# An expert's gather and add over 128 rows instead of 104, with the ranks dealt over the partitions

## The chip, the core and the metric

The kernel runs on one core of one Trainium2 chip. The metric is device time in microseconds (us), the median of several runs. Engines are called PE (TensorE matmul), PEld (its weight loads), DVE (VectorE), ACT (ScalarE), POOL (GpSimd) and SP (SyncE). DMAs issued on SP go through the hardware queue q1, those issued on POOL through the software queue q0; both are worked off by the same 16 transfer engines.

## What is computed

One layer on 1,024 tokens of width 1,024 in float32: an input projection, a stick-breaking attention and a gated recurrence side by side, an output projection, and then a mixture of 32 experts, on which the change bears. A router gives every token two experts; the tokens of an expert are gathered, run through the expert, weighted and added back:

```
grp = argmax(softmax(x2 @ w_rg + b_rg)); in_grp = (x2 @ w_re + b_re)[group grp]
top_val, top_idx = top_k(in_grp, 2); gate = softmax(top_val) * p_grp
for each block of an expert's tokens:
    xb = x2[tok]
    hb = silu(xb @ w_gate[e]) * (xb @ w_up[e])        # 1024 -> 512
    y[tok] += (hb @ w_down[e]) * gate                 # 512 -> 1024
out = rmsnorm(h + y) * g_final
```

With the reference's inputs the 2,048 assignments give an expert between 41 and 82 tokens, 64 on average (counted by running the reference's router); expert 0 has 76, expert 30 has 56, expert 31 has 66.

## The kernel before

**Slots.** Every expert has `C = 104` slots. `place` (L832 on) works out the rank of each token among those of its expert, and a one-hot comparison of the rank with `iota` (L844) turns it into a slot: slot number = rank = partition. `idx[slot, e]` then holds the token's row number; a slot that no token has holds 1024. Gather and add name all 104 slots, with `bounds_check=T - 1` and `oob_is_err=False`, so that rows with 1024 are skipped. A branch at L1142 runs extra blocks if an expert has more than `C` tokens; it isn't taken here.

**Weights.** An expert has six pieces of 1 MB (two of gate, two of up, two of down), each 128 partitions x 8 KB. SP loads them at L761 into a ring of 18 pieces (`NA + NB_`), paced so that at most three are in flight: the fourth waits for the first to land. Since float32 products are made of three fp32r products, each half piece is split into a high and a low part, ACT at L1045 and DVE at L1046, 12 splits an expert, 384 in all; PE then runs three matmuls on each at L1069 to L1071.

**Experts.** One expert is 72 matmuls of 512 columns and 12 transposes: 8 turn the gathered rows `xg` (L1025), 4 the hidden rows `hb` (L1058). The gather of expert e+2 is issued on POOL (L1016) when the transposes of expert e have read their buffer, the add of expert e (L1062, `compute_op=ALU.add` into the output) when ACT has written its `y` (L1127). A scheduler puts each engine's instructions in order.

**End.** When the add of expert 30 has landed, SP loads the eight output tiles back (L1213), ACT squares and sums them (L1206), POOL and DVE finish the norm, SP stores (L1216). The rows of expert 31 go another way: gathered (L1016), added (L1217), normed and scattered (L1219).

Of the kernel before, what the change touches and what calls it, by code (L numbers as in the profile page):

```python
# [7 lines left out]
F32 = mybir.dt.float32  # L8
# [10 lines left out]
P = 128  # L19
# [14 lines left out]
def kernel(  # L34
# [26 lines left out]
    def pool(name, bufs, side="left", **kw):  # L61
        return tc.tile_pool(name=name, bufs=bufs, side=side, reuse_waits="tile", **kw)
# [35 lines left out]
        return v[:, 1, :]  # L98


    NE, NG, EG, C = 32, 4, 8, 104
    rt = ctx.enter_context(pool("rt", 1))
    iota = rt.tile([P, P], F32, name="iota")
    nc.gpsimd.iota(iota, pattern=[[1, P]], base=0, channel_multiplier=0, allow_small_or_imprecise_dtypes=True)
# [727 lines left out]
    def place(i, A, As, at):  # L832

        V = nc.vector
        rp = bank("tr")
        nc.tensor.matmul(rp[:, :NE], lhsT=ones, rhs=asum, start=True, stop=False)
        nc.tensor.matmul(rp[:, :NE], lhsT=tri, rhs=As, start=False, stop=True)
        tv = wk.tile([P, 2, NE], F32R, name="tv", bufs=1)
        V.tensor_scalar(tv, A, tokb[:, i:i + 1], None, op0=ALU.mult)
        jk = wk.tile([P, 2, NE], F32, name="rj", bufs=1)  # L840
        V.tensor_tensor(jk, A, rp[:, None, :NE].to_broadcast([P, 2, NE]), op=ALU.mult)
        V.tensor_reduce(rank[:, i, :], jk, axis=AX.X, op=ALU.add)
        ohs = wk.tile([P, 2, C], F32R, name="soh", bufs=1)
        V.tensor_tensor(ohs, iota[:, None, :C].to_broadcast([P, 2, C]), rank[:, i, :, None].to_broadcast([P, 2, C]), op=ALU.is_equal)  # L844
        if i < NT - 1:
            gv = gates(i, A, *at)
            V.tensor_add(asum, asum, As.bitcast(F32))
        yield 900
        tp = bank("tr")
        for j in range(2):  # L850
            nc.tensor.matmul(tp[:C, :NE], lhsT=ohs[:, j], rhs=tv[:, j], start=j == 0, stop=j == 1)
        if i == 0:
            V.tensor_copy(tab[:C, 0, :], tp[:C, :NE])
        elif i < NT - 1:
            V.tensor_add(tab[:C, 0, :], tab[:C, 0, :], tp[:C, :NE])
        else:
            V.scalar_tensor_tensor(idx[:C], tp[:C, :NE], float(T), tab[:C, 0, :], op0=ALU.add, op1=ALU.add)
            gv = gates(i, A, *at)
            V.tensor_add(asum, asum, As.bitcast(F32))
        gp = bank("tr")  # L860
        for j in range(2):
            nc.tensor.matmul(gp[:C, :NE], lhsT=ohs[:, j].bitcast(F32), rhs=gv[:, j], start=j == 0, stop=j == 1)
        if i == 0:
            V.tensor_copy(tab[:C, 1, :], gp[:C, :NE])
        else:
            V.tensor_add(tab[:C, 1, :], tab[:C, 1, :], gp[:C, :NE])
        yield 430
# [142 lines left out]
    for t in xgs:  # L1010
        nc.scalar.activation(t, zero.to_broadcast([P, D]), AF.Copy)

    spl = ctx.enter_context(pool("spl", 3))

    def gather(dst, src, ix):
        nc.gpsimd.indirect_dma_start(out=dst, out_offset=None, in_=src,  # L1016
                                     in_offset=bass.IndirectOffsetOnAxis(ap=ix, axis=0),
                                     bounds_check=T - 1, oob_is_err=False)
# [7 lines left out]
            yield h, pt[:, :, :C]  # L1026

    def gather_in(e):
        gather(xgs[e % NX][:C], mrows[:, :], idx[:C, e:e + 1])

    def expert_in(e):
        mH, mL = [], []
# [13 lines left out]
        nc.vector.tensor_sub(wl, w, wh.bitcast(F32))  # L1046
        return wh, wl

    def hidden(gps, ups, **kw):
        hb = ex.tile([P, 4, P], F32, name="hb", **kw)[:C]  # L1050
        nc.scalar.activation(hb, gps.rearrange("t (p k) -> t k p", k=4), AF.Silu)
        nc.vector.tensor_tensor(hb, ups.rearrange("t (p k) -> t k p", k=4), hb, op=ALU.mult)
        return hb
# [35 lines left out]
    def run_steps(upto):  # L1089

        for n in range(live.get("n", 0), min(upto + AHEAD, len(steps) + AHEAD)):
            live["n"] = n + 1
            if n < len(steps):
                first, e, c = steps[n]
                if first:
                    w = pieces[6 * e + 2 * (c // 4) + c % 2][:, 2 * (c // 2 % 2):2 * (c // 2 % 2) + 2, :]
                else:
                    w = pieces[6 * e + 4 + c % 2][:, :, 512 * (c // 2):512 * (c // 2) + 512]
                halves.append(split(w))
            if n >= AHEAD:  # L1100
                step(*steps[n - AHEAD], *halves.pop(0))

    def step(first, e, c, wh, wl):
        if first:
            if c == 0:
                live["g"], live["u"] = bank("pj")[:C], bank("z")[:C]
                load_until(min(6 * e + NA + NB_, 6 * NE))
            if c == 4 and e + 1 < NE:
                mHL.append(expert_in(e + 1))
            three(live["gu"[c % 2]], *mHL[e], wh, wl, 2 * (c // 2), KD - 1)  # L1110
            if c == 7:
                live["hb"] = hidden(live["g"], live["u"])
            if (c == 1 - (e == NE - 1) and 0 < e) or (c == 7 and e == NE - 1):
                pt = turn_hidden(live["hb"])
                hH = live["hH"] = ex.tile([P, 4, C], F32R, name="hH")
                hL = live["hL"] = ex.tile([P, 4, C], F32R, name="hL")
                nc.scalar.activation(hH, pt, AF.Copy)  # L1117
                nc.vector.tensor_sub(hL, pt, hH.bitcast(F32))
        else:
            if c == 0:  # L1120
                live["y"] = ex.tile([P, D], F32, name="y", bufs=2)[:C]
            if c % 2 == 0:
                live["yps"] = bank("o")[:C]
            three(live["yps"], [live["hH"]], [live["hL"]], wh, wl, 2 * (c % 2), 3)
            if c % 2 == 1:
                h = slice(256 * (c - 1), 256 * (c - 1) + 512)
                nc.scalar.activation(live["y"][:, h], live["yps"], AF.Copy, scale=tab[:C, 1, e:e + 1])  # L1127
            if c == 3 and e < NE - 1:
                add_rows(live["y"], idx[:C, e:e + 1])

    run_steps(12)
    most = rt.tile([P, 1], F32, name="most")
    nc.vector.tensor_reduce(most, cnt, axis=AX.X, op=ALU.max)
# [6 lines left out]
    NR = -(-T // C) - 1  # L1140
    NB = NR * NE
    with tc.If(biggest > C):  # L1142
        bb = ex.tile([P, 2, NR, NE], F32, name="bb", tag="emL0", bufs=2)
        nc.gpsimd.iota(bb[:, 0], pattern=[[C, NR], [0, NE]], base=C, channel_multiplier=0, allow_small_or_imprecise_dtypes=True)
        nc.gpsimd.iota(bb[:, 1], pattern=[[0, NR], [1, NE]], base=0, channel_multiplier=0, allow_small_or_imprecise_dtypes=True)
        flags = xgs[(NE - 1) % NX].bitcast(I32)[:, :2 * NR * NE].rearrange("p (a r e) -> p a r e", a=2, r=NR)
        nc.vector.tensor_tensor(flags[:, 0], cnt[:, None, :].to_broadcast([P, NR, NE]), bb[:, 0], op=ALU.is_gt)
        nc.vector.tensor_copy(flags[:, 1], bb[:, 1])
        bf = bb.rearrange("p a r e -> p a (r e)")
        fl = flags.rearrange("p a r e -> p a (r e)")  # L1150
        flying.clear()
        with tc.For_i(0, NB, 1) as b:
            wanted = nc.values_load(fl[0:1, 0, bass.ds(b, 1)], min_val=0, max_val=1)
            with tc.If(wanted > 0):
                ev = nc.values_load(fl[0:1, 1, bass.ds(b, 1)], min_val=0, max_val=NE - 1,
                                    engines=[mybir.EngineType.SP])
                cur = ex.tile([P, 2], F32, name="cur")
                nc.vector.tensor_copy(cur, bf[:, :, bass.ds(b, 1)].rearrange("p a b -> p (a b)"))
                mine = ex.tile([P, 2, NT * 2], F32, name="mine")
                nc.vector.tensor_scalar(mine[:, 0], eid.rearrange("p i j -> p (i j)"), cur[:, 1:2], None, op0=ALU.is_equal)  # L1160
                nc.vector.tensor_scalar(mine[:, 1], rank.rearrange("p i j -> p (i j)"), cur[:, 0:1], None, op0=ALU.subtract)
# [20 lines left out]
                    for q, ps in ((0, gps), (1, ups)):  # L1182
                        nc.tensor.matmul(ps, lhsT=mT[k // 4][:, k % 4], rhs=ws[2 * (k // 4) + q][:, k % 4, :], start=k == 0, stop=k == KD - 1)
                hT = ex.tile([P, 4, C], F32, name="hT", tag="hH")
                nc.scalar.activation(hT, turn_hidden(hidden(gps, ups, tag="y", bufs=2)), AF.Copy)
                y = ex.tile([P, D], F32, name="y", bufs=2)[:C]
                for h in range(2):
                    c = slice(512 * h, 512 * h + 512)
                    yps = bank("o")[:C]
                    for k in range(4):  # L1190
                        nc.tensor.matmul(yps, lhsT=hT[:, k, :], rhs=ws[4 + k // 2][:, k % 2, c], start=k == 0, stop=k == 3)
                    nc.scalar.activation(y[:, c], yps, AF.Copy, scale=bt[:C, 1:2])
                add_rows(y, bi[:C, 0:1])


    run_steps(len(steps))
# [17 lines left out]
    for i in range(NT):  # L1214
        last_norm(zs[i], P)
        nc.sync.dma_start(out2[P * i:P * i + P], zs[i][:, 0])  # L1216
    nc.vector.tensor_add(z[:C, 0], z[:C, 0], live["y"])  # L1217
    last_norm(z, C)
    nc.gpsimd.indirect_dma_start(out=out2, out_offset=bass.IndirectOffsetOnAxis(ap=own, axis=0), in_=z[:C, 0], in_offset=None,  # L1219
                                 bounds_check=T - 1, oob_is_err=False)  # L1220
# [30 lines left out]
```

## Time and profile before

| | |
|---|---|
| median of 3 runs | 1387.79 us (1384.51 to 1390.88) |
| profiled execution, its own time | 1399.36 us |
| its span, first to last instruction | 1397.6 us |
| mean granted clock of PE | 0.975 |
| PE busy | 1287.0 us (92%) |
| DVE / ACT / POOL busy | 1066.3 (76%) / 843.5 (60%) / 278.2 us (20%) |
| q1 / q0, share of 16 engines' span | 49.7% / 8.1% |

The experts run from about 760 us to 1375 us of the span. Matmuls overlap in the trace: their recorded durations of about 400 ns are longer than the 231 to 233 ns from one start to the next. The share of DMA is the mean of the 16 engines; of a queue, the time that its packets took as a share of 16 engines' time.

### The profile page before, as it was taken

The page shows a single profiled execution, that of the slowest core. Times are in us where ns is not written, and L with a number is a line of the kernel's source. Part 1 is how long each engine was busy: PE and PEld are TensorE (multiplying, and loading weights), DVE is VectorE, ACT ScalarE, POOL GpSimd, SP SyncE. Part 2 cuts the span into 40 slices and gives each one's busy share as a digit, 9 for nine tenths or more (in the row PEclk, how much of TensorE's full clock was granted, in tenths as well). Part 3 has the DMA queues.
Part 4 walks back from the last instruction along what each step waited for, and adds up shares of the span by engine and source line. Part 5 has one row for each costly group of instructions (what it writes and reads, how often), then busy time and mean ns, then how long its engine had stood idle before and what let it go on. Part 6 is the DMA issues. An engine that isn't in the chain of part 4 may idle for free. (4 is left out here: it accounts for less than half of the span.)

```text
span 1397.6 us, 19149 instructions
## 1 busy us (share of the span) xinstructions
PE 1287.0 (92%) x6812; PEld 1020.8 (73%) x6813; DVE 1066.3 (76%) x1675; ACT 843.5 (60%) x1371; POOL 278.2 (20%) x364
## 2 busy tenths in 40 slices
PE   6999889988998899989994999999999999999992
PEld 5888788868886888777884677777777666676761
DVE  5474887489747975897674798888888888788884
ACT  5333653365425643663232788888888778788874
POOL 3202330133003410232011111111111111111114
PEclk9999999999999999999995899999999999999996
DMA  6111001101110101554888689999999999999977
GB/s 198 46 31 46 20 23 35 48 26 30 34 38 27 35 23 31 178 183 135 286 277 274 226 301 341 343 346 354 356 340 355 334 338 359 346 361 346 358 288 256
DMA packets 84370, 278.63 MB, mean 199 GB/s; under 512 B 12870, under 2 KB 45662, under 8 KB 59696
## 3 DMA queue, kind: packets, MB, share of 16 engines
q1 hardware_dynamic: 70624, 245.63, 49.7%
q0 software_dynamic: 13648, 31.76, 8.1%
q8 instruction: 54, 0.88, 0.3%
q14 instruction: 44, 0.36, 0.1%
HBM read 255.47 MB, written 32.51 MB: 206 GB/s over the span
## 5 line engine op out<-in xcount | busy, mean ns | idle before, releaser
L1046 DVE TENSOR_TENSOR wl<-w,wh 128x1024 fp32r<-128x1024 f32 x384 | 456.4, 1221 | 73.5 <-ACT wh L1045 72.9
L1045 ACT ACTIVATE wh<-w 128x1024 fp32r<-128x1024 f32 x384 | 402.4, 1058 | 86.1 <-PE z L1071 26.2
L199 PE MATMUL pj<-aH,whi 128*128 128x346 f32 (+4 forms) x576 | 207.6, 361 | 0.8 <-ACT aH L156 0.5
L200 PE MATMUL pj<-aL,whi 128*128 128x346 f32 (+4 forms) x576 | 203.3, 353 | 1.1 <-DVE aL L157 1.0
L201 PE MATMUL pj<-aH,wlo 128*128 128x346 f32 (+4 forms) x576 | 201.4, 350 | 0.0
L200 PEld LDWEIGHTS pj<-aL,whi 128*128 128x128 f32 x576 | 109.4, 190 | 7.6 <-DVE aL L157 1.7
L199 PEld LDWEIGHTS pj<-aH,whi 128*128 128x128 f32 x576 | 109.3, 190 | 7.8 <-ACT aH L156 1.2
L201 PEld LDWEIGHTS pj<-aH,wlo 128*128 128x128 f32 x576 | 109.3, 190 | 7.0
L1069 PE MATMUL z<-wh,emH 128*104 128x512 f32 x256 | 104.4, 408 | 7.7 <-ACT wh L1045 7.7
L1069 PE MATMUL pj<-wh,emH 128*104 128x512 f32 x256 | 106.0, 414 | 2.2 <-ACT wh L1045 2.2
L1016 POOL DMA_INDIRECT xg<-mrows,idx x32 | 43.1, 1348 | 317.6 <-PE tr L1025 301.0
L1070 PE MATMUL pj<-wl,emH 128*104 128x512 f32 x256 | 105.5, 412 | 0.7 <-DVE wl L1046 0.4
L1069 PE MATMUL o<-wh,hH 128*104 128x512 f32 x256 | 102.3, 400 | 3.3 <-ACT hH L1117 3.3
L1070 PE MATMUL o<-wl,hH 128*104 128x512 f32 x256 | 104.4, 408 | 1.0 <-DVE wl L1046 1.0
L321 DVE TENSOR_TENSOR_SCAN keep<-keep,small 128x144 f32<-128x144 f32 (+3 forms) x64 | 90.2, 1409 | 17.2 <-POOL keep L317 16.7
L1070 PE MATMUL z<-wl,emH 128*104 128x512 f32 x256 | 102.7, 401 | 0.0
L1071 PE MATMUL pj<-wh,emL 128*104 128x512 f32 x256 | 102.1, 399 | 0.0
L1071 PE MATMUL z<-wh,emL 128*104 128x512 f32 x256 | 102.0, 398 | 0.0
L1071 PE MATMUL o<-wh,hL 128*104 128x512 f32 x256 | 101.1, 396 | 0.0
L1062 POOL DMA_INDIRECT out_dram<-y,idx x31 | 49.9, 1609 | 193.2 <-ACT y L1127 176.4
L344 ACT ACTIVATE wH<-tr 128x512 fp32r<-128x512 f32 (+1 forms) x80 | 44.7, 560 | 60.1 <-PE tr L341 57.0
L341 PE MATMUL tr<-ident,beta 128*128 128x128 f32 x288 | 50.9, 281 | 21.7 <-DVE beta L322 17.0
(270 smaller groups left out, 2578.1 us busy)
## 6 DMA issues: line engine op xcount, KB each, us to landing
w<-in_w_expert_gate_dram SPq DMA_DIRECT2D x64, 1024.0 KB, 9.4
w<-in_w_expert_up_dram SPq DMA_DIRECT2D x64, 1024.0 KB, 9.7
w<-in_w_expert_down_dram SPq DMA_DIRECT2D x64, 1024.0 KB, 9.8
wraw<-in_w_in_dram SPq DMA_DIRECT2D x28, 512.0 KB, 3.9
out_dram<-ht POOLq DMA_DIRECT2D x12, 512.0 KB, 4.5
xt<-in_x_dram SPq DMA_DIRECT2D x8, 512.0 KB, 4.4
wraw<-in_w_out_dram SPq DMA_DIRECT2D x8, 512.0 KB, 4.8
mxt<-mixed SPq DMA_DIRECT2D x16, 256.0 KB, 4.9
```

The costliest lines, as they stand in the source:

```text
L199: nc.tensor.matmul(ps[:, :n], lhsT=hi[:, k], rhs=aH[:, k, c0:c0 + n], start=k == 0, stop=False)
L200: nc.tensor.matmul(ps[:, :n], lhsT=hi[:, k], rhs=aL[:, k, c0:c0 + n], start=False, stop=False)
L201: nc.tensor.matmul(ps[:, :n], lhsT=lo[:, k], rhs=aH[:, k, c0:c0 + n], start=False, stop=k == KD - 1)
L321: nc.vector.tensor_tensor_scan(kr, kr, zero.to_broadcast([P, S]), 1.0, op0=ALU.mult, op1=ALU.add)
L341: nc.tensor.transpose(pt[:, q, :], beta[2 * p + u, h][:, c:c + P], ident)
L344: nc.scalar.activation(hi[:, :n], pt[:, :n], AF.Copy)
L1045: nc.scalar.activation(wh, w, AF.Copy)
L1046: nc.vector.tensor_sub(wl, w, wh.bitcast(F32))
L1062: nc.gpsimd.indirect_dma_start(out=out2, out_offset=bass.IndirectOffsetOnAxis(ap=ix, axis=0), in_=y, in_offset=None, bounds_check=T - 1, o ...
L1069: nc.tensor.matmul(ps, lhsT=hi, rhs=wh[:, u], start=k + u == 0, stop=False)
L1070: nc.tensor.matmul(ps, lhsT=hi, rhs=wl[:, u], start=False, stop=False)
L1071: nc.tensor.matmul(ps, lhsT=lo, rhs=wh[:, u], start=False, stop=k + u == last)
```

## The change

`C` becomes 96. Gather and add of the experts now name 128 rows: `idx` has 1024 in its last 32 partitions, written once, so that those are skipped; `xg` is gathered whole and `y` is two tiles kept for the whole stage, whose last 32 partitions are zeroed once. A new table `slot` gives the partition its rank: the one-hot compares ranks with `slot` instead of `iota`, so that partition p holds rank `slot[p]`. In the first 64 partitions, runs of four partitions alternate between low ranks (below 64) and high ranks (64 to 95); partitions 64 to 95 hold low ranks only. Of partitions p and p + 32, for p from 0 to 31 and from 64 to 95, exactly one holds low ranks. The code of the extra blocks is fitted to the new tiles and still isn't run. The last gather and scatter, of expert 31's rows, name 96 rows.

```diff
-    NE, NG, EG, C = 32, 4, 8, 104
+    NE, NG, EG, C = 32, 4, 8, 96
...
-        V.tensor_tensor(ohs, iota[:, None, :C].to_broadcast([P, 2, C]), rank[:, i, :, None].to_broadcast([P, 2, C]), op=ALU.is_equal)
+        V.tensor_tensor(ohs, slot[:, None, :].to_broadcast([P, 2, C]), rank[:, i, :, None].to_broadcast([P, 2, C]), op=ALU.is_equal)
...
+    slot = wk.tile([P, C], F32, name="slot", bufs=1)
+    near = slot[:, :64].rearrange("p (e d c b) -> p e c d b", e=2, d=4, c=2)
+    for e in range(2):
+        for c in range(2):
+            nc.gpsimd.iota(near[:, e, c], pattern=[[2, 4], [16 if e == c else 8, 4]], base=c if e == c else 64 + c, channel_multiplier=0,
+                           allow_small_or_imprecise_dtypes=True)
+    nc.gpsimd.iota(slot[:, 64:].rearrange("p (d b) -> p d b", b=4), pattern=[[1, 8], [16, 4]], base=8, channel_multiplier=0,
+                   allow_small_or_imprecise_dtypes=True)
+    nc.vector.tensor_scalar(idx[C:], ones[C:, :NE], float(T), None, op0=ALU.mult)
...
+    ys = [ex.tile([P, D], F32, name=f"y{u}") for u in range(2)]
...
-        gather(xgs[e % NX][:C], mrows[:, :], idx[:C, e:e + 1])
+        gather(xgs[e % NX], mrows[:, :], idx[:, e:e + 1])
...
-                live["y"] = ex.tile([P, D], F32, name="y", bufs=2)[:C]
+                live["y"] = ys[e % 2]
...
-                nc.scalar.activation(live["y"][:, h], live["yps"], AF.Copy, scale=tab[:C, 1, e:e + 1])
+                nc.scalar.activation(live["y"][:C, h], live["yps"], AF.Copy, scale=tab[:C, 1, e:e + 1])
             if c == 3 and e < NE - 1:
-                add_rows(live["y"], idx[:C, e:e + 1])
-
+                add_rows(live["y"], idx[:, e:e + 1])
+
+    for t in ys:
+        nc.scalar.activation(t[C:], zero[C:].to_broadcast([P - C, D]), AF.Copy)
```

POOL, between the attention's last blocks (`tri` is a mask for the ranks, `wr` the router's weights):

```order
 L959 DMA out_dram<-ht 128x1024
 L994 AFFINE_SELECT tri<-ones 128x128
+L1000 IOTA slot 128x4x4 x4
+L1002 IOTA slot 128x32
 L706 MEMSET wr 128x320
```

Five instructions that write `slot` stand between two that were neighbours.

ACT before, at the start of the experts (`mT` and `dv` belong to the router, `small` is the source of zeros):

```order
L820 ACTIVATE dv<-dv 128x2
L1011 ACTIVATE xg_7784<-small 128x1024
L1011 ACTIVATE xg_7785<-small 128x1024
L1045 ACTIVATE wh<-w 128x1024 x3
L1036 ACTIVATE emH_7802<-tr 128x416
L1036 ACTIVATE emH_7811<-tr 128x416
L1045 ACTIVATE wh<-w 128x1024 x4
```

ACT now, at the same place:

```order
L820 ACTIVATE dv<-dv 128x2
L1021 ACTIVATE xg_7791<-small 128x1024
L1021 ACTIVATE xg_7792<-small 128x1024
L1143 ACTIVATE y_7795<-small 32x1024
L1143 ACTIVATE y_7796<-small 32x1024
L1057 ACTIVATE wh<-w 128x1024 x2
L1048 ACTIVATE emH_7811<-tr 128x384
L1057 ACTIVATE wh<-w 128x1024
L1048 ACTIVATE emH_7820<-tr 128x384
L1057 ACTIVATE wh<-w 128x1024 x4
```

Two zeroings of `y` stand ahead of the first split, and the third split has moved behind the first copy of turned rows.

POOL before, from the last row of the router to the first add:

```order
L886 DMA mrows<-mt 128x1024
L1016 DMA xg_7784<-mrows,idx 104x1024
L1016 DMA xg_7785<-mrows,idx 104x1024
L1016 DMA xg_7784<-mrows,idx 104x1024
L1016 DMA xg_7785<-mrows,idx 104x1024
L1016 DMA xg_7784<-mrows,idx 104x1024
L1062 DMA out_dram<-y,idx 1024x1024
```

POOL now:

```order
L886 DMA mrows<-mt 128x1024
L1028 DMA xg_7791<-mrows,idx 128x1024
L1028 DMA xg_7792<-mrows,idx 128x1024
L1028 DMA xg_7791<-mrows,idx 128x1024
L1028 DMA xg_7792<-mrows,idx 128x1024
L1028 DMA xg_7791<-mrows,idx 128x1024
L1073 DMA out_dram<-y_7795,idx 1024x1024
```

Gathers and adds keep their places; their size is 128 rows.

## Rows read from the trace of the kernel before

**Rows 1.** Stretches: length, busy of PE, PEld, DVE, ACT, POOL, clock, DMA, GB/s

```profile
900.00:1000.00 100.00, 100.00 (x467) 70.85 (x466) 89.44 (x90) 84.24 (x100) 16.12 (x11) 1.00 0.99 355
...
1100.00:1200.00 100.00, 95.55 (x430) 67.65 (x429) 83.06 (x83) 77.64 (x92) 14.46 (x10) 0.97 1.00 345
1200.00:1300.00 100.00, 95.80 (x439) 67.69 (x438) 83.55 (x84) 79.32 (x95) 16.12 (x11) 0.98 0.99 355
1300.00:1350.00 50.00, 48.19 (x222) 33.99 (x221) 43.49 (x44) 40.56 (x48) 6.18 (x5) 1.00 0.98 358
```

**Rows 2.** L1045 in 800 to 1100, then 1100 to 1340: count, ns min/median/max, times

```profile
L1045 ACT ACTIVATE wh<-w x199: 1044/1061/1072, 800.2 to 1098.8; 128x1024 fp32r<-128x1024 f32 x199
...
L1045 ACT ACTIVATE wh<-w x150: 1038/1061/1071, 1100.5 to 1339.3; 128x1024 fp32r<-128x1024 f32 x150
```

**Rows 3.** Waits from 1100 to 1365: us in total, times, longest

```profile
PE z L1069 <- ACT wh L1045: 7.7, 5, 2.6
...
ACT wh L1045 <- DMA w<-in_w_expert_up_dram: 10.5, 6, 2.6
```

**Rows 4.** L761, 800 to 1100, then 1100 to 1340; SP's waits, 800 to 1100

```profile
L761 SPq DMA_DIRECT2D w<-in_w_expert_up_dram x30: 327/328/383, 800.2 to 1088.7; - x30
...
L761 SPq DMA_DIRECT2D w<-in_w_expert_up_dram x25: 327/328/328, 1102.6 to 1335.5; - x25
...
SPq L761 <- DMA w<-in_w_expert_down_dram: 89.7, 28, 6.7
```

**Rows 5.** DMA queues (packets, MB, share) from 1200.7 to 1206, then 1218.5 to 1228.5

```profile
q1 hardware_dynamic: 275, 2.03, 96.7%
q0 software_dynamic: 1, 0.00, 0.0%
...
q1 hardware_dynamic: 481, 3.49, 92.1%
```

**Rows 6.** DMA queues during two gathers: 1186.2 to 1192.4, 1206.2 to 1210.8

```profile
q1 hardware_dynamic: 215, 1.55, 83.5%
q0 software_dynamic: 142, 0.29, 18.1%
...
q1 hardware_dynamic: 171, 1.23, 81.9%
q0 software_dynamic: 133, 0.26, 20.1%
```

**Rows 7.** DMA queues during an add: 1195.1 to 1200.6

```profile
q1 hardware_dynamic: 220, 1.59, 71.6%
q0 software_dynamic: 143, 0.34, 31.1%
```

**Rows 8.** First gather: timeline of POOL and PE, and stretch 757 to 770

```profile
759.98 2.03 POOL L1016 DMA_INDIRECT xg<-mrows,idx  x1 [6.46 <-DVE wl L1046]
...
770.40 1.62 PE L1025 MATMUL tr<-ident,xg 104*128 104x104 f32 x8 [12.55 <-DMA xg<-mrows,idx]
...
757.00:770.00 13.00, 0.85 (x5) 0.71 (x4) 4.22 (x7) 2.95 (x3) 3.12 (x2) 0.50 0.78 253
```

**Rows 9.** Transposes of 104 columns: four in the timeline; group, 800 to 1100

```profile
1346.65 0.52 PE L1058 MATMUL tr<-ident,hb 104*128 104x104 f32 x4
...
L1058 PE MATMUL tr<-ident,hb 104*128 104x104 f32 x68 | 8.8, 252 | 0.0
```

**Rows 10.** Timeline of the end, POOL, SP and ACT

```profile
1357.00 1.60 POOL L1062 DMA_INDIRECT out_dram<-y,idx  x1 [12.30 <-ACT y L1127]
...
1363.29 3.98 SPq L1213 DMA_DIRECT2D w<-out_dram  x8
...
1367.03 1.06 ACT L1206 ACTIVATE w<-w 128x1024 f32<-128x1024 f32 x1 [2.76 <-DMA w<-out_dram]
...
1368.08 0.50 ACT L1117 ACTIVATE hH<-tr 128x416 fp32r<-128x416 f32 x1
```

**Rows 11.** POOL groups and timeline; ACT timeline at the experts' start

```profile
L104 POOL IOTA iota<- 128x128 f32 x1 | 0.2, 238 | 0.4 <-POOLq L1237 0.4
...
611.35 0.29 POOL L315 TENSOR_SCALAR_AFFINE_SELECT beta<-beta 128x128 f32<-128x128 f32 x1 [2.35 <-ACT beta L312]
...
754.42 1.98 ACT L1011 ACTIVATE xg<-small 128x1024 f32<-128x1024 f32 x2
757.51 2.95 ACT L1045 ACTIVATE wh<-w 128x1024 fp32r<-128x1024 f32 x3 [1.10 <-PE tr L862]
```

More of the change, by code (lines that the diff above doesn't have):

```diff
@@ L1047, in split, with hidden @@
         return wh, wl
-    def hidden(gps, ups, **kw):
-        hb = ex.tile([P, 4, P], F32, name="hb", **kw)[:C]
+    def hidden(gps, ups, hb):
         nc.scalar.activation(hb, gps.rearrange("t (p k) -> t k p", k=4), AF.Silu)
@@ L1111, in step @@
             if c == 7:
-                live["hb"] = hidden(live["g"], live["u"])
+                live["hb"] = hidden(live["g"], live["u"], ex.tile([P, 4, P], F32, name="hb")[:C])
             if (c == 1 - (e == NE - 1) and 0 < e) or (c == 7 and e == NE - 1):
@@ L1142 @@
     with tc.If(biggest > C):
-        bb = ex.tile([P, 2, NR, NE], F32, name="bb", tag="emL0", bufs=2)
-        nc.gpsimd.iota(bb[:, 0], pattern=[[C, NR], [0, NE]], base=C, channel_multiplier=0, allow_small_or_imprecise_dtypes=True)
-        nc.gpsimd.iota(bb[:, 1], pattern=[[0, NR], [1, NE]], base=0, channel_multiplier=0, allow_small_or_imprecise_dtypes=True)
+        bb = [ex.tile([P, NR, NE], F32, name=f"bb{u}", tag=f"emL{u}", bufs=2) for u in range(2)]
+        nc.gpsimd.iota(bb[0], pattern=[[C, NR], [0, NE]], base=C, channel_multiplier=0, allow_small_or_imprecise_dtypes=True)
+        nc.gpsimd.iota(bb[1], pattern=[[0, NR], [1, NE]], base=0, channel_multiplier=0, allow_small_or_imprecise_dtypes=True)
         flags = xgs[(NE - 1) % NX].bitcast(I32)[:, :2 * NR * NE].rearrange("p (a r e) -> p a r e", a=2, r=NR)
-        nc.vector.tensor_tensor(flags[:, 0], cnt[:, None, :].to_broadcast([P, NR, NE]), bb[:, 0], op=ALU.is_gt)
-        nc.vector.tensor_copy(flags[:, 1], bb[:, 1])
-        bf = bb.rearrange("p a r e -> p a (r e)")
+        nc.vector.tensor_tensor(flags[:, 0], cnt[:, None, :].to_broadcast([P, NR, NE]), bb[0], op=ALU.is_gt)
+        nc.vector.tensor_copy(flags[:, 1], bb[1])
+        bf = [t.rearrange("p r e -> p (r e)") for t in bb]
         fl = flags.rearrange("p a r e -> p a (r e)")
@@ L1157 @@
                 cur = ex.tile([P, 2], F32, name="cur")
-                nc.vector.tensor_copy(cur, bf[:, :, bass.ds(b, 1)].rearrange("p a b -> p (a b)"))
+                for u in range(2):
+                    nc.vector.tensor_copy(cur[:, u:u + 1], bf[u][:, bass.ds(b, 1)])
                 mine = ex.tile([P, 2, NT * 2], F32, name="mine")
@@ L1184 @@
                 hT = ex.tile([P, 4, C], F32, name="hT", tag="hH")
-                nc.scalar.activation(hT, turn_hidden(hidden(gps, ups, tag="y", bufs=2)), AF.Copy)
-                y = ex.tile([P, D], F32, name="y", bufs=2)[:C]
+                nc.scalar.activation(hT, turn_hidden(hidden(gps, ups, ys[1][:C, :512].rearrange("p (a b) -> p a b", b=P))), AF.Copy)
+                y = ys[0]
                 for h in range(2):
@@ L1191 @@
                         nc.tensor.matmul(yps, lhsT=hT[:, k, :], rhs=ws[4 + k // 2][:, k % 2, c], start=k == 0, stop=k == 3)
-                    nc.scalar.activation(y[:, c], yps, AF.Copy, scale=bt[:C, 1:2])
-                add_rows(y, bi[:C, 0:1])
+                    nc.scalar.activation(y[:C, c], yps, AF.Copy, scale=bt[:C, 1:2])
+                add_rows(y[:C], bi[:C, 0:1])
     run_steps(len(steps))
@@ L1216 @@
         nc.sync.dma_start(out2[P * i:P * i + P], zs[i][:, 0])
-    nc.vector.tensor_add(z[:C, 0], z[:C, 0], live["y"])
+    nc.vector.tensor_add(z[:C, 0], z[:C, 0], live["y"][:C])
     last_norm(z, C)
```

## The prediction

> **What bounds the kernel now.** I read first the busy time by stretches. From 900 to 1000 us PE is busy for all of the 100 us; from 1100 on it is not, although nothing else about the work has changed: 95.55 and 95.80 of 100 us, 48.19 of 50, and the granted clock falls to 0.97 and 0.98 [rows 1]. That is 4.5 + 4.2 + 1.8 = 10.5 us idle, and 3 + 2 = 5 us given away in the clock: 15.5 us. The splits tell the same. ACT makes one every (1098.8 - 800.2) / 198 = 1.508 us before 1100 and every (1339.3 - 1100.5) / 149 = 1.603 us after it [rows 2], or 18.1 and 19.2 us for the 12 of an expert; 149 x 0.095 = 14.1 us are lost. So the experts' stage has two halves: PE bounds the first, something else the second.
>
> The waits name it. After 1100 PE waits for the split and the split for a weight piece [rows 3]. SP in turn spends its time on the landing of earlier pieces, its pacing rule, long before that [rows 4]. Its issues give the rate: three kinds of 30 make 90 pieces in 300 us, 3.33 us each and 20.0 us an expert; then 74 in 240 us, 3.24 and 19.5 us [rows 4]. From 800 to 1100 us, 199 / 2 = 99.5 pieces are used up and 90 come in [rows 2, 4]. The ring's stock thus shrinks by 9.5 pieces, which are 9.5 x 18.1 / 6 = 28.7 us of PE's work, and then there is none. **The weight stream is slower than PE from the start, and PE feels it when the stock is gone.**
>
> What the stream loses, the queues show. Between two bursts of rows q1 moves 2.03 MB in 5.3 us and 3.49 MB in 10 us [rows 5]. A weight packet is 8 KB, so these are 248 and 426 packets, together 44.0 a us; an expert's 768 would take 17.4 us, less than PE's 18.1. In two gathers q1 moves 1.55 MB in 6.2 us and 1.23 MB in 4.6 us [rows 6]: 189 and 150 packets where 273 and 202 would have gone, so a gather costs the stream 84 / 44 = 1.9 and 52 / 44 = 1.2 us, 1.55 us on average. In an add 194 packets go in 5.5 us instead of 242 [rows 7]: 1.1 us. The sum, 17.4 + 1.55 + 1.1 = 20.05 us, is what SP's issues gave.
>
> **Why a gather costs more than an add.** Share x 16 x time / packets gives the time of one packet. A weight packet takes 331 and 346 ns in the quiet stretches, 325 ns beside an add, but 438 and 402 ns beside a gather [rows 5 to 7]. A gathered row of 4 KB takes 253 and 233 ns where half a quiet weight packet would be 168; an added row takes 330. The add moves more bytes of memory and disturbs nobody; the gather alone writes into the partitions, as the weights do. So I put the loss down to writes of several engines into the same group of partitions. And the bursts are long: four rows on each of 16 engines, each behind a weight packet, would be over in 4 x (0.33 + 0.325) = 2.6 us for the add, eight on one engine in 5.2; the add lasted 5.5 [rows 7]. So the 64 or so ranks lie on about half of the engines.
>
> The Trainium skill has a rule for that, in "DMA: Bandwidth & Descriptors", section "Why a DMA increments its semaphore by 16 and not by 1": a transfer uses the largest number of engines, 16 at most, that divides its slowest dimension, so 13 for 104 rows and 16 for 128; and in "The descriptor swizzle" a transfer of 128 partitions gives each engine four neighbours and the four that lie 32 further on. By it the new table gives every engine four low ranks, and its rows lie in the partitions that it writes for the weights too; a gather would then cost the 0.67 us worked out below, without it 1.55. The long bursts agree with the first rule; nothing in the trace shows which partition an engine serves.
>
> **The change part by part.** *Gather and add.* If rows no longer cross, a gather costs what its 64 rows take at the quiet pace, 64 x 0.168 / 16 = 0.67 us an expert; the other end is 1.55, nothing gained. I take 0.8, near the lower end, since the add's rows show what a transfer costs that crosses nobody: 1.1 us, even less than 64 x 0.330 / 16 = 1.3. The add stays at 1.1 (0.9 to 1.3). Evenness may also fill idle engines, which were busy for 96.7% and 92.1% in the quiet stretches [rows 5]: 0 to 0.7 us, I take 0.2. The stream then needs 17.4 + 0.8 + 1.1 - 0.2 = 19.1 us an expert (18.3 to 20.05). With 18.0 us on PE the deficit is 1.1 us, and the stock of 28.7 us lasts 26 of the 29 experts after 800 us; the later pace was 0.5 us better, so the last three cost 0.6 us each. Some 2 us of the 15.5 remain: **gain 13.5 us**. With half of the relief (19.55) the stock lasts 18 experts and about 10 us remain; with none, all 15.5.
>
> *Slots.* Matmuls move 512 columns as before. The 12 transposes of an expert move 96 columns for 104: one step is (0.52 - 0.252) / 3 = 0.09 us [rows 9], 8/104 of it 7 ns, so 12 x 31 x 7 ns = **2.6 us**, which counts where PE is the bound.
>
> *First gather.* PE stands still for 12.55 us until the first gather has landed; the instruction ends at 762.01, the rows land 8.4 us later [rows 8]. Eight rows behind eight weight packets are 8 x (0.24 + 0.42) = 5.3 us of that. Expert 0 has 76 tokens, so about five rows an engine, 3.3 us: 2 us sooner. Writing 128 rows for 104 adds 24/104 of 2.03, 0.5 us. PE runs at half clock there [rows 8], so the saving may count less: **1.2 us** (0 to 2). Such writing on POOL costs nothing later, where a gather comes an expert or more ahead.
>
> *Last add.* SP's loads of the output are issued 1363.29 - 1358.60 = 4.7 us after the add of expert 30 was written; ACT waits 2.76 us for them with the last `hH` queued behind, and PE for that [rows 10]. Four rows instead of eight at 0.33 us are 1.3 us, less 0.4 for the writing: **0.9 us**.
>
> *What is added.* Five iotas of 0.24 us stand on POOL ahead of `wr` and the masks of the attention; POOL then waited 2.35 us for ACT [rows 11], so they are covered, and 1.2 us without that cover. The zeroing of two `y`, as long as that of `xg`, 2 us in all, delays the first split by 0.9, since ACT waited 1.10 us there [rows 11]; PE's wait for the gather covers that and the third split's new place. The fill of `idx` stands at the program's start behind loads.
>
> Sum: 13.5 + 2.6 + 1.2 + 0.9 = 18.2 us, from the profiled execution's own 1399.4 us (span 1397.6) to 1381.2. The median of the runs is 11.6 us below that execution. If the profile adds them everywhere alike, the median comes to 1369.6. If it adds them to the stream, then the stall in a plain run is only 15.5 - 11.6 = 3.9 us and the median comes to 1387.8 - 3.9 - 4.7 = 1379.2. No row decides; I take the middle, **1375 us**.
>
> **The rivals.** *The stream stays as slow.* If what a gather costs lies in the memory and not in the partitions, it costs 1.55 us wherever its rows go. Then only the ends gain, 1.2 + 0.9 us, since a faster PE merely empties the ring sooner: 1385.7 us. For it speaks that the gather reads scattered rows; against it that the add, which reads and writes such rows, leaves weight packets at 325 ns [rows 7]. Chance 0.20.
>
> The Trainium skill states in "SBUF — State Buffer", section "A bandwidth-pool intuition that's wrong (but worth ruling out)", about 358 GB/s between memory and one core. By it the sum of bytes would bound the stream, and dealing rows could not help; the trace disagrees, with 2.03 MB in 5.3 us, 383 GB/s, in a quiet stretch [rows 5].
>
> *The change doesn't do what it says.* If engines take neighbours by eights, partitions 64 to 95 still put eight low ranks on one engine, bursts stay long and rows cross: again about 1386 us. Chance 0.09.
>
> *Slower.* Now every gathered row could lie where its own engine writes weights. If the slowdown to 402 to 438 ns comes from two queues of one engine that write side by side, and not from crossing, more packets than before are slowed. With a gather at twice its cost, 3.1 us, the stream falls 1.55 us an expert further behind over 29 experts: 45 us less 4.7, about 1428 us. It is slower than before by more than 7 us once a gather costs (7 + 2.1) / 29 = 0.3 us more, 1.85 us. The place is every gather of the stage. Against it: in the add two queues of one engine alternate too, without that. Chance 0.05.
>
> **How the numbers follow.** Forecast 0.66, its own range 1365 to 1382; the two cases near 1386 together 0.29, slower 0.05. The range that should hold 8 times in 10 reaches from 1365 to 1387: it leaves out about 0.05 below, half of the cases at 1386, which spread over 1382 to 1390, and the slower one. About 0.5%, 6.9 us, is what a measurement here can tell from no change. Faster by more: 0.66, almost all of the forecast and a little of the others; same: 0.28; slower: 0.06.
>
> **What would show it.** PE busy for 100 of 100 us from 1100 to 1300; a split every 1.50 us there; 80 or more pieces issued in 240 us; bursts of rows of about 3 us; weight packets under 360 ns beside a gather; PE's wait for the first gather near 11 us. I am wrong if weight packets beside a gather still take over 400 ns, or if the bursts are short and PE waits for splits all the same.

## The result, and the profile after

The changed kernel takes **1368.03 us** (median, 1364.28 to 1369.55) against 1389.13 us for the kernel before in the same comparison (1384.51 to 1390.88): a ratio of 0.985, with a 95% interval from 0.982 to 0.988, 21 us. The forecast was 1375 us, faster, within 1365 to 1387. The profiled execution has 1367.73 us of its own and a span of 1366.0 us.

PE's stretches after, beside [rows 1] (columns: stretch, length, then busy us and instructions of PE, PEld, DVE, ACT and POOL, granted clock, DMA share, GB/s):

```profile
1100.00:1200.00 100.00, 99.79 (x473) 68.48 (x472) 89.52 (x90) 84.46 (x102) 16.02 (x11) 1.00 1.00 378
1200.00:1300.00 100.00, 100.00 (x469) 68.58 (x468) 90.07 (x90) 84.44 (x101) 15.56 (x10) 1.00 0.95 364
```

The idle time of the second half is gone, and so is the fall of the clock. The splits and the issues of the weights, beside [rows 2, 4] (the splits are now L1057; count, shortest/median/longest ns, first and last start):

```profile
L1057 ACT ACTIVATE wh<-w x202: 1042/1062/1072, 799.4 to 1099.5; 128x1024 fp32r<-128x1024 f32 x101
...
L1057 ACT ACTIVATE wh<-w x146: 1042/1062/1072, 1099.5 to 1319.0; 128x1024 fp32r<-128x1024 f32 x146
...
L761 SPq DMA_DIRECT2D w<-in_w_expert_gate_dram x34: 327/328/425, 802.1 to 1099.5; - x34
L761 SPq DMA_DIRECT2D w<-in_w_expert_down_dram x34: 327/328/328, 802.9 to 1091.0; - x34
L761 SPq DMA_DIRECT2D w<-in_w_expert_up_dram x33: 327/328/382, 810.6 to 1096.5; - x33
...
SPq L761 <- DVE wl L1058: 47.1, 35, 4.7
```

A split comes every 300.1 / 201 = 1.493 us up to 1100 and every 219.5 / 145 = 1.514 us behind it. From 800 to 1100 us, 101 pieces are used up and 34 + 34 + 33 = 101 come in, where 90 came in before: the ring stays full, and SP now waits 47.1 us for DVE to free a piece (12.9 before).

The queues, beside [rows 5 to 7]: a stretch between two bursts (1033.3 to 1040.0), a gather of 74 rows (1040.0 to 1043.2) and an add (1047.1 to 1050.5); packets, MB, share of 16 engines:

```profile
q1 hardware_dynamic: 381, 2.83, 100.3%
...
q1 hardware_dynamic: 148, 1.07, 79.5%
q0 software_dynamic: 138, 0.30, 23.5%
...
q1 hardware_dynamic: 137, 0.98, 69.9%
q0 software_dynamic: 135, 0.21, 32.6%
```

With 8 KB a packet, 2.83 MB in 6.7 us are 51.6 weight packets a us (46.8 and 42.6 in the two stretches of [rows 5]), 311 ns each. In the gather 131 go in 3.2 us, 312 ns each ([rows 6]: 438 and 402): the gather costs the stream (165 - 131) / 51.6 = 0.66 us, and lasts 3.2 us where the two of before lasted 6.2 and 4.6. In the add 120 go in 3.4 us, where 175 would have gone: 1.1 us, as before. These are single stretches; averages over many follow with the experiments.

Where the time went, by the first split of experts 1 and 31: 783.5 and 1341.4 us before, 771.2 and 1311.3 after. The start gained 12.3 us, the thirty experts between 557.9 - 540.1 = 17.8, the end 1.5; together the 31.6 us by which the spans differ. The medians differ by only 21.1, so 10 us of this belong to one execution; the second profile below says which.

### The profile page after: what moved, and what is told of

It reads as the page before. It is cut to its first block, busy times and chain, and to the rows that moved or that the text cites. A ratio compares the mean times of both kernels' runs of the same rounds, so it can differ in the third digit from the quotient of the medians.

```text
span 1366.0 us, 19155 instructions
## 1 busy us (share of the span) xinstructions
PE 1271.6 (93%) x6812; PEld 994.9 (73%) x6813; DVE 1062.9 (78%) x1676; ACT 843.8 (62%) x1373; POOL 279.1 (20%) x369
## 5 line engine op out<-in xcount | busy, mean ns | idle before, releaser
L1057 ACT ACTIVATE wh<-w 128x1024 fp32r<-128x1024 f32 x384 | 403.0, 1059 | 71.0 <-PE pj L1082 24.7
L1080 PE MATMUL pj<-wh,emH 128*96 128x512 f32 x256 | 104.6, 409 | 2.2 <-DVEq L1155 2.2
L1081 PE MATMUL o<-wl,hH 128*96 128x512 f32 x256 | 103.8, 406 | 1.9 <-DVE wl L1058 1.9
L1081 PE MATMUL pj<-wl,emH 128*96 128x512 f32 x256 | 104.7, 409 | 0.4 <-DVE wl L1058 0.4
L321 DVE TENSOR_TENSOR_SCAN keep<-keep,small 128x144 f32<-128x144 f32 (+3 forms) x64 | 90.2, 1409 | 17.6 <-POOL keep L317 17.2
L1080 PE MATMUL z<-wh,emH 128*96 128x512 f32 x256 | 103.5, 404 | 0.0
L1080 PE MATMUL o<-wh,hH 128*96 128x512 f32 x256 | 101.5, 397 | 1.8 <-ACT hH L1128 1.8
L1081 PE MATMUL z<-wl,emH 128*96 128x512 f32 x256 | 101.3, 396 | 0.0
L1082 PE MATMUL pj<-wh,emL 128*96 128x512 f32 x256 | 101.1, 395 | 0.0
L1082 PE MATMUL o<-wh,hL 128*96 128x512 f32 x256 | 101.1, 396 | 0.0
L1082 PE MATMUL z<-wh,emL 128*96 128x512 f32 x256 | 101.0, 395 | 0.0
L191 ACT ACTIVATE whi<-wraw 128x1024 fp32r<-128x1024 f32 x28 | 29.9, 1069 | 67.9 <-PE pj L200 45.2
```

Of the source, the lines that this page charges most:

```text
L321: nc.vector.tensor_tensor_scan(kr, kr, zero.to_broadcast([P, S]), 1.0, op0=ALU.mult, op1=ALU.add)
L1057: nc.scalar.activation(wh, w, AF.Copy)
L1080: nc.tensor.matmul(ps, lhsT=hi, rhs=wh[:, u], start=k + u == 0, stop=False)
L1081: nc.tensor.matmul(ps, lhsT=hi, rhs=wl[:, u], start=False, stop=False)
L1082: nc.tensor.matmul(ps, lhsT=lo, rhs=wh[:, u], start=False, stop=k + u == last)
```

## The experiments

**The kernel before a second time.** No edit.

> The kernel before, unchanged, profiled a second time, for the start of the experts (first split of expert 1 at 783.5 us before, 771.2 after, where I had put 1.2 us). If the start is a matter of the program, PE's wait for the first gather is again within 1 us of 12.55, the clock is at half for 35 to 40 us there, and expert 1's first split is within 2 us of 783.5. If it hangs on how one weight piece and the first rows meet in one execution, the wait and that split move by 3 us or more. Its own time: near 1389 if the 11.6 us by which the first profile lies over its median were chance, near 1399 if the profile adds them.

Its own time was 1390.21 us, its span 1388.5. POOL's first gather, PE's first transposes, and two stretches:

```profile
753.47 1.96 POOL L1016 DMA_INDIRECT xg<-mrows,idx  x1 [6.39 <-DVE wl L1046]
...
759.17 1.62 PE L1025 MATMUL tr<-ident,xg 104*128 104x104 f32 x8 [7.90 <-DMA xg<-mrows,idx]
...
1100.00:1200.00 100.00, 92.40 (x422) 65.28 (x420) 81.75 (x81) 77.31 (x91) 14.67 (x11) 0.98 0.99 345
1200.00:1300.00 100.00, 95.03 (x435) 66.38 (x435) 82.87 (x83) 78.59 (x94) 15.27 (x10) 1.00 1.00 348
```

PE waited 7.90 us, not 12.55 [rows 8], the granted clock stood at half, 1.2 GHz, for 17 us around it, not 38, and expert 1's first split came at 771.2 us, not 783.5, exactly where it comes after the change. Most of those 12.3 us are a matter of the execution. The stall of the second half stays: 7.6 + 5.0 us idle in these 200 us. Against this profile the change gains nothing up to expert 1, 560.2 - 540.1 = 20.1 us from there to expert 31 and 2.3 at the end, 22.5 us, which agrees with the medians. The first profile of before was unlucky in its start and typical in its stall.

**The slots in order, 128 rows named.** Of the change, the dealing is taken back:

```diff
-    near = slot[:, :64].rearrange("p (e d c b) -> p e c d b", e=2, d=4, c=2)
...
+    nc.gpsimd.iota(slot, pattern=[[1, C]], base=0, channel_multiplier=0, allow_small_or_imprecise_dtypes=True)
```

> After with the slots in order (partition = rank): gather and add still name 128 rows, the tokens again lie in the first 64 partitions or so. Crossing theory (a gather slows the weights only where an engine writes rows into partitions that another engine serves): with 128 rows named the rows don't cross, so weight packets beside a gather stay under 350 ns and a gather costs the stream 0.9 us or less, although its rows lie on half of the engines and a burst lasts 4 to 5.5 us; PE stays busy for 99 of 100 us from 1100 to 1300; time within 6 us of after's 1368. Evenness theory (the cost is that half of the engines are held up by eight rows each): weight packets over 400 ns, a gather costs 1.4 us or more, the ring's stock runs out, PE idles after 1150 us; time 1378 to 1386.

**96 rows named, dealt by sixes.** The dealing stays, in another pattern; the 32 further rows go:

```diff
+    six = slot.rearrange("p (k j) -> p k j", j=6)
+    nc.gpsimd.iota(six[:, :, :4], pattern=[[1, 16], [16, 4]], base=0, channel_multiplier=0, allow_small_or_imprecise_dtypes=True)
+    nc.gpsimd.iota(six[:, :, 4:], pattern=[[1, 16], [16, 2]], base=64, channel_multiplier=0, allow_small_or_imprecise_dtypes=True)
...
-        gather(xgs[e % NX], mrows[:, :], idx[:, e:e + 1])
+        gather(xgs[e % NX][:C], mrows[:, :], idx[:C, e:e + 1])
...
-                add_rows(live["y"], idx[:, e:e + 1])
+                add_rows(live["y"][:C], idx[:C, e:e + 1])
```

> After with 96 rows named in gather and add in place of 128, and a slot table that gives every six neighbouring partitions four low ranks and two high ones. If 96 rows go to 16 engines in sixes, the rows are even but cross, since weights go to the engines in fours. Crossing theory: bursts of 3 us or less, yet weight packets over 400 ns beside a gather, a gather costs 1.2 us or more; time 1376 to 1386. Evenness theory: bursts of 3 us, weight packets under 350 ns, a gather costs 0.9 us or less; time within 6 us of after's 1368. Bursts of 4.5 us or more would say that 96 rows aren't taken in sixes, and then this run tells the two apart in nothing.

**C = 96 and nothing else.**

```diff
-    NE, NG, EG, C = 32, 4, 8, 104
+    NE, NG, EG, C = 32, 4, 8, 96
```

> Before with C = 96 and nothing else: 96 rows in order, no table, no row zeroed. It bears the part of the gain that lies in the smaller number alone. Both theories: transposes give 2.6 us where PE is the bound; the tokens lie on 11 of 16 engines, six rows each, so bursts are three quarters as long, some 3.8 us. Crossing theory: weight packets over 400 ns beside a gather, a gather costs 1.3 to 1.5 us, PE idles after 1150 us; time 1380 to 1386. Evenness theory: a gather costs 1.0 to 1.2 us, the stock lasts nearly to the end; time 1374 to 1379.

The three took 1370.96, 1369.65 and 1371.69 us, ratios of 0.987 (0.984 to 0.991), 0.988 (0.985 to 0.992) and 0.987 (0.984 to 0.991) to before: **each has the whole gain**, as far as this can be measured, the last with one number changed. In none of them is PE idle for more than 0.3 us of the 200 from 1100 to 1300. For the time, both theories fell: each expected 1374 us or more of two of the three.

For the packets, one held. The same gather of 74 rows and the quiet stretch ahead of it; first the slots in order (1037.6 to 1043.8, 1043.8 to 1047.4), then sixes (1030.9 to 1038.4, 1038.4 to 1041.8), then C = 96 alone (1036.8 to 1044.4, 1044.4 to 1047.6):

```profile
q1 hardware_dynamic: 296, 2.15, 96.1%
...
q1 hardware_dynamic: 155, 1.14, 78.4%
q0 software_dynamic: 136, 0.30, 21.1%
```

```profile
q1 hardware_dynamic: 429, 3.12, 99.8%
...
q1 hardware_dynamic: 111, 0.78, 74.0%
q0 software_dynamic: 106, 0.30, 30.5%
```

```profile
q1 hardware_dynamic: 394, 2.88, 96.6%
...
q1 hardware_dynamic: 101, 0.71, 75.1%
q0 software_dynamic: 104, 0.30, 29.2%
```

Worked out as above, a weight packet beside the gather takes 324 ns with the slots in order and 312 after the change, where 128 rows are named, but 423 with sixes and 443 with C = 96 alone. The slowdown follows the 128 rows and not the evenness, as the crossing theory says. But the quiet stretches, which I had taken to be alike, differ: 42.3 weight packets a us with the slots in order, 46.3 with C = 96 alone, 50.8 with sixes, 51.6 after. That follows the evenness, though single stretches scatter (those of before gave 46.8 and 42.6). So there are two effects, and PE hides how large each is.

**The stream by itself.** To see the stream, PE's work was cut: the third of the three products of every weight row (low part of the token rows x high part of the weights) is left out, in five kernels alike.

```diff
-            nc.tensor.matmul(ps, lhsT=hi, rhs=wl[:, u], start=False, stop=False)
-            nc.tensor.matmul(ps, lhsT=lo, rhs=wh[:, u], start=False, stop=k + u == last)
+            nc.tensor.matmul(ps, lhsT=hi, rhs=wl[:, u], start=False, stop=k + u == last)
```

Before, cut so:

> Before without the third of the three products of every weight row (low part of the token rows x high part of the weights), so that PE has 48 matmuls an expert for 72 and some 12.1 us of work; loads, splits, gathers and adds stay. Now the weight stream should bound the stage, with DVE next (89 of 100 us at 18.0 us an expert is 16.1). Once the ring is used up, the pace of the splits is the pace of the stream. By the bursts of rows: 768 packets at 45.2 a us are 17.0, a gather 1.58, an add 1.22: 19.8 us an expert. Rival: the bursts are no measure of it, since the packets between them are held down by the ring while it is full, and all five of these kernels run at one pace, within 0.3 us.

C = 96 alone, cut so:

> The kernel with C = 96 alone, without the third product. By the bursts: 768 / 47.4 = 16.2, a gather 1.51, an add 1.17: 18.9 us an expert. If crossing of rows were all that counts, the gather would cost as in before and the pace would be 19.6 or more; if the load of the engines were all, the pace would lie between that of before and that of after in the ratio of the longest row counts, 8, 6 and 4 to 5: 18.8. Rival of one pace: within 0.3 us of before's.

128 rows with the slots in order, cut so:

> The kernel with 128 rows named and the slots in order, without the third product: rows don't cross, but lie on half of the engines. By the bursts: 768 / 45.5 = 16.9, a gather 0.79, an add 1.28: 18.95 us an expert. If evenness were all that counts: before's 19.8. Rival of one pace: within 0.3 us of before's.

After, cut so:

> After without the third product: even and not crossing. By the bursts 768 / 46.9 = 16.4, a gather 0.57, an add 1.11: 18.1 us an expert; but there the ring was full and held the stream to PE's 18.0, so the pace alone may be lower, down to DVE's 16.1 or so; I take 17.5. The whole kernel is then some 2.0 to 2.3 us an expert faster than before's without the third product, 50 us in all. Rival of one pace: within 0.3 us of before's.

And, in a later comparison, the sixes:

> The kernel with 96 rows dealt by sixes, without the third product (low part of the token rows x high part of the weights): even, but crossing. By the bursts of the full kernel: 768 / 49.3 = 15.6, a gather 1.28, an add 1.21: 18.1 us an expert once the ring is used up, 1345 us or so in all. If crossing and unevenness each cost about 1.1 us an expert and add, as the paces of 20.0 (both), 18.9 (either less) and at most 17.6 (neither) say, the pace lies near 18.6 to 18.8, and the time near 1355. If evenness were all, the pace would be that of the changed kernel, 17.6 or less, 1335.

The issues of the weights from 950 to 1250 us, first of before, then of after, both cut:

```profile
L761 SPq DMA_DIRECT2D w<-in_w_expert_up_dram x30: 327/328/328, 950.9 to 1236.5; - x30
L761 SPq DMA_DIRECT2D w<-in_w_expert_gate_dram x30: 327/328/328, 953.4 to 1246.8; - x30
L761 SPq DMA_DIRECT2D w<-in_w_expert_down_dram x30: 327/328/328, 961.4 to 1242.3; - x30
```

```profile
L761 SPq DMA_DIRECT2D w<-in_w_expert_down_dram x35: 327/328/328, 951.1 to 1248.9; - x35
L761 SPq DMA_DIRECT2D w<-in_w_expert_gate_dram x34: 327/328/328, 956.6 to 1243.9; - x34
L761 SPq DMA_DIRECT2D w<-in_w_expert_up_dram x34: 327/328/328, 959.1 to 1246.4; - x34
```

Six pieces are an expert: 6 x (1246.8 - 950.9) / 89 = 19.95 us for before, 6 x (1248.9 - 951.1) / 102 = 17.5 for after. The other three, read alike:

| cut kernel | rows on the engines | weight packet beside a gather shown (mean), uncut | stream, us an expert | whole, us |
|---|---|---|---|---|
| before | eight each on eight | 438, 402 (422) ns | 19.95 | 1393.11 |
| 128 rows, slots in order | eight each on eight | 324 (348) ns | 19.0 | 1364.29 |
| C = 96 alone | six each on eleven | 443 (417) ns | 19.0 | 1364.35 |
| 96 rows, sixes | four or five on each | 423 (421) ns | 17.95 | 1332.92 |
| after | four or five on each | 312 (329) ns | 17.5 | 1334.94 |

The means are over all weight packets that start within a gather that stands alone, from 800 to 1310 us. How the rows lie was not seen; it is what follows if 104 rows go to 13 engines by eights and 96 to 16 by sixes, and if of 128 rows each of 16 engines gets four neighbours and the four that lie 32 further on. The mean lengths of the uncut bursts, in the order of the table, agree for the gathers (5.0, 4.2, 4.1, 2.9 and 2.7 us) and in the main for the adds (5.0, 5.4, 4.0, 3.2 and 4.0).

Before, cut, is no faster than uncut (1393.11 and 1392.37 us in one comparison), with a third of PE's matmuls on the weights gone: PE's work doesn't set its time. The bursts had foretold four of the five paces within 0.15 us, and for after the value below theirs was the right one; the rival of one pace fell. For the sixes, the bursts' 18.1 held and the sum of two equal effects (18.6 to 18.8) fell. **Evenness is the larger effect**: 2.0 us an expert where rows cross (19.95 to 17.95), 1.5 where they don't. The first pair also differs in the rows named, 104 and 96; with 96 named in both, from six on an engine to four or five, it is 1.05. Naming 128 rows, so that they don't cross, gives 0.9 with uneven rows and 0.4 with even ones.

Most of the evenness is gained between the bursts. Over all stretches between bursts from 950 to 1250 us, the cut kernels move 45.0 and 44.1 weight packets a us with eight rows on an engine (before, slots in order), at 346 and 347 ns each, 47.0 at 336 with six, and 49.6 and 48.6 at 321 and 328 with four or five (sixes, after). An expert's 768 packets then take 17.1 and 17.4 us against 15.5 and 15.8: 1.6 us either way.

The last two kernels come out level because both still had pieces in stock nearly to expert 28; their splits kept almost the same pace, (1225.8 - 1017.5) / 12 = 17.36 and (1229.6 - 1021.7) / 12 = 17.33 us an expert from 16 to 28.

**After and C = 96 alone, side by side.**

> The changed kernel once more, beside C = 96 alone on the same chip. If the weight stream no longer bounds anything, the table and the 32 further rows bring nothing over C = 96 alone: the two medians lie within 4 us (0.3%). If they do bring something (a shorter first gather and last add), after is 4 to 8 us faster. Its start (expert 1's first split) may lie anywhere from 769 to 776 us, as in the five profiles but the first of before.

> C = 96 alone once more, beside after on the same chip: 1368 to 1372 us, within 4 us of it if the dealing brings nothing as long as PE is the bound; 4 to 8 us slower otherwise. The lead of the pieces over their use falls again from some 40 us to about 10 us at the end of the stage, as 18.9 us of stream against 18.0 of PE over 30 experts would have it (27 us).

1370.46 us (ratio to before 0.988, 0.986 to 0.989) for after and 1368.02 (0.987, 0.985 to 0.989) for C = 96 alone. The table and the 32 further rows bring nothing that can be measured, as long as PE is the bound. C = 96 alone ends with a smaller reserve: a piece is issued 39 us ahead of its use at expert 6 and 15 us ahead at expert 31, where after keeps 38 to 40 us throughout. Expert 1's first split came at 769.0 us in after and at 772.2 in C = 96 alone; in the profiles of uncut kernels, the first one of before left out, it lies between 769.0 and 775.7.

**84 slots.** On top of the change, with the ranks dealt anew:

```diff
-    NE, NG, EG, C = 32, 4, 8, 96
+    NE, NG, EG, C = 32, 4, 8, 84
...
+    for at, pattern, base in ((slice(0, 32), [[1, 32]], 0), (slice(64, C), [[1, C - 64]], 32), (slice(32, 64), [[1, 8], [8, 4]], C - 32)):
+        nc.gpsimd.iota(slot[:, at], pattern=pattern, base=base, channel_multiplier=0, allow_small_or_imprecise_dtypes=True)
```

> After with 84 slots (an expert has at most 82 tokens here): 128 rows named, ranks 0 to 31 in the first 32 partitions, 32 to 51 in partitions 64 to 83, 52 to 83 dealt by eights over partitions 32 to 63. It measures the term of the transposes and is a candidate for a faster kernel. By the prediction's working (7 ns for 8 columns, 12 transposes, 31 experts) 12 columns fewer give 3.9 us. By PE's pace from expert 1 to 16, 18.16 us an expert with 104 columns and 18.04 with 96, 0.015 us a column: 5.6 us. So 1362 to 1365 where after gives 1368. Rival: the load of the engines is less even (5 to 6 rows on eight of them, 4 on five, none on three), the stream falls to 19 us an expert against 17.85 on PE, the ring's stock of 28 us is used up before the end and PE idles: no gain, or 2 to 5 us lost.

1374.84 us (0.990, 0.988 to 0.991): slower than after. Two stretches, and the waits of PE and ACT from 1150 to 1320 us (engine, line, what for: us in total, times, longest):

```profile
1000.00:1100.00 100.00, 100.00 (x471) 64.15 (x470) 89.32 (x90) 83.65 (x101) 15.56 (x11) 1.00 1.01 382
...
1200.00:1300.00 100.00, 95.24 (x433) 59.64 (x432) 81.61 (x82) 77.56 (x94) 14.12 (x10) 1.00 0.93 351
...
PE pj L1075 <- ACT wh L1052: 3.3, 14, 0.3
PE pj L1076 <- DVE wl L1053: 2.5, 8, 0.3
...
ACT wh L1052 <- PE z L1077: 12.9, 25, 0.6
```

Up to expert 23 the gain is there; from expert 1 to 16 it is (1038.6 - 770.0) / 15 = 17.91 us an expert, after 18.04, which is 12 columns at 0.011 us. From about 1165 us on the pace is 19.1 and then 19.5. The rival that I had named isn't it: pieces are issued 42 us ahead of their use at expert 28, and neither ACT nor PE waits for a weight DMA. PE and ACT wait for each other, PE for a split, ACT for a split buffer, of which there are three. What sets this off at 1165 us stays open.

## Why the prediction was right, and which terms were off

**The bound, right.** The stream was slower than PE, the ring hid that until 1100 us, and it no longer is: PE is busy for 99.79 and 100.00 of 100 us, 101 pieces come in where 90 did, and no split waits for a piece. The forecast left 2 of the 15.5 us of stall; none remained.

**The gather, right.** 0.8 us was put down for it, 0.66 measured in the gather shown, and 0.57 on average over those from 800 to 1310 us. The cause, rows that cross into partitions of other engines, is borne out in so far as the slowdown comes and goes with the number of rows named, at the same bytes, rows and memory; which engine writes which partition was not seen.

**Evenness, mis-sized.** This is the step that was wrong. I took 0.2 us from the idle share in two quiet stretches [rows 5], with 0.7 as the upper end; it measures 1.5 to 2.0. The error was to price a quiet packet at the 331 to 346 ns of before wherever it stood, and the quiet pace as a constant of the stream. In the quiet stretch shown with the slots in order, 2.15 MB are 262 weight packets, and 96.1% of 16 x 6.2 us gives each 364 ns; in that of after it is 311. On average over the cut kernels it is 346 and 347 ns with eight rows on an engine, 321 and 328 with four or five. By these and the rates above, the engines' idle share falls from 3 and 4% to under 1%, which is 0.4 to 0.7 us of the 1.6, the size that the forecast had in view; the shorter packets, which it left out, give the other 0.9 to 1.2. So the stream came out at 17.5 us, not 19.1, and what carried the argument, the crossing, is the smaller part.

The time doesn't show this error, since PE is the bound once the stream keeps up. The cut kernels also answer what half of the relief is worth: I had put 10 us of stall for it, at 19.55 us an expert. With the crossing gone and the rows uneven the stream takes 19.0, and 1.0 us of deficit times 29 experts is just the stock of 28.7 us. So either effect was enough, and so is the number 96 alone, which leaves the crossing and comes to 19.0 with six rows on an engine instead of eight.

**The transposes, low.** The step of 7 ns is there (252 ns in [rows 9], now 245):

```profile
L1037 PE MATMUL tr<-ident,xg 96*128 96x96 f32 x132 | 16.3, 245 | 0.0
```

PE's pace from expert 1 to 16 went from 18.16 to 18.04 us: 0.12 an expert, 3.7 us over 31, for 2.6.

**The first gather, low, and the start misread.** The pair of profiles gives 12.3 us where 1.2 stood. Beside the second profile of before, the stretch from the first split of all to expert 1's is 20.3 us, and 17.5 and 16.6 in the two of after: about 3 us. C = 96 alone, whose rows aren't dealt, has 17.6 and 17.2, so that these 3 us are not shown to come from fewer rows on an engine. POOL's first gather and the transposes it feeds, after:

```profile
754.50 1.13 POOL L1028 DMA_INDIRECT xg<-mrows,idx  x1 [6.11 <-issue]
...
758.37 1.51 PE L1037 MATMUL tr<-ident,xg 96*128 96x96 f32 x8 [5.89 <-DMA xg<-mrows,idx]
```

PE's wait was 5.89 us, not the 11 of the forecast, and writing 128 rows took 1.13 us, not 2.5. The rest is the scatter of one execution, and makes up most of the 11.6 us by which the profile of before lay over the median. I took the middle between two readings of these, 1375; they lay in neither the stall nor everywhere but in the start, so that taking them off whole, 1381.2 - 11.6 = 1369.6, would have come within 2 us of the measured 1368.03.

**The last add, low.** The end, beside [rows 10]:

```profile
1327.40 1.56 POOL L1073 DMA_INDIRECT out_dram<-y,idx  x1 [12.78 <-ACT y L1138]
...
1332.26 3.78 SPq L1227 DMA_DIRECT2D w<-out_dram  x8
...
1335.93 1.06 ACT L1220 ACTIVATE w<-w 128x1024 f32<-128x1024 f32 x1 [1.22 <-DMA w<-out_dram]
```

The loads are issued 1332.26 - 1328.96 = 3.3 us after the add was written (4.7), ACT waits 1.22 us (2.76): 1.5 us for the 0.9 forecast. The 0.4 us taken off for writing 128 rows wasn't needed, 1.56 us for 1.60.

**What was hidden stayed hidden.** The iotas stand on POOL as 0.49 + 0.18 us, less than the 1.2 put down, ahead of a wait for ACT that is now 1.75 us (2.35 in [rows 11]):

```profile
608.02 0.49 POOL L1000 IOTA slot<- 128x16 f32 x4
608.48 0.18 POOL L1002 IOTA slot<- 128x32 f32 x1
...
610.73 0.29 POOL L315 TENSOR_SCALAR_AFFINE_SELECT beta<-beta 128x128 f32<-128x128 f32 x1 [1.75 <-ACT beta L312]
```

**The rivals.** That memory sets the price of a gather is out: the same rows cost 312 ns a weight packet in one kernel and 443 in another. After, cut, moves 392 GB/s over 250 us:

```profile
1000.00:1250.00 250.00, 217.15 (x867) 114.79 (x868) 229.03 (x232) 214.40 (x260) 50.09 (x29) 1.00 1.01 392
```

The Trainium skill's figure of about 358 GB/s between memory and one core ("SBUF — State Buffer", section "A bandwidth-pool intuition that's wrong (but worth ruling out)") isn't a bound here.

That the change doesn't do what it says is out, by gathers of 2.7 us on average and adds of 4.0, where the slots in order, eight on an engine, gave 4.2 and 5.4. Eights of neighbours would have put eight low ranks on each of four engines with the new table too. The Trainium skill has 16 engines for 128 rows, each with four neighbours and four 32 further on ("DMA: Bandwidth & Descriptors", sections "Why a DMA increments its semaphore by 16 and not by 1" and "The descriptor swizzle"); the trace agrees by the shorter bursts. Why an add of after takes longer than one with sixes, 3.2 us, stays open.

That two queues of one engine hinder each other as the slower rival has it is out: in 18 of the 26 gathers of after that stand alone, a weight packet takes 309 to 313 ns. One of the others has 394; seven, of 1.2 to 1.7 us, fall where few weight packets go, 20 to 37 in each, and these take 430 to 695. After, cut, where the ring isn't full, has none above 328 ns from 950 to 1250 us.

## What to carry to other kernels

A stream that falls behind slowly needs only as much relief as its stock has to bridge: first work out that deficit, then look for the cheapest edit that covers it; here one number did, and the table bought reserve that no kernel with the whole of PE's work used. To see what two edits to a hidden stream are worth, cut the work that hides it, and read the stream's own pace. And before an odd start or end of one profile enters a sum, compare the profile with the median, and if they disagree, look at a second execution.

## What the runs showed of the hardware

- Small rows on a few engines slow a large stream that uses all of them, also between the bursts: in the cut kernels 45.0 and 44.1 weight packets a us with eight rows on an engine, 49.6 and 48.6 with four or five; the whole stream loses 1.5 to 2.0 us an expert. How many rows each engine has is inferred, not seen. Why a packet then takes 346 ns rather than 321 to 328 wasn't tried; that a piece lands with its slowest engine, and SP waits for pieces that landed, would explain the idle share and not the longer packet.
- A gather that names 96 or 104 rows slows weight packets beside it to 417 to 422 ns on average; one that names 128 leaves them at 348 with the slots in order and at 309 to 313 in 18 of 26 gathers of after.
- In the two executions of before, PE's wait for the first gather was 12.55 and 7.90 us, and expert 1's first split came 12.3 us apart.
